# Output weights staged in freed operand slots, and their decode rows gathered into four events

## The chip, the cores and the metric

The kernel runs on one core of a Trainium2 chip, as one program and one launch. The metric is the device time of that core in microseconds (us). Engines are named as in the profile: PE is TensorE (matmuls), PEld its weight loads, DVE is VectorE, ACT is ScalarE, POOL is GpSimd and SP is SyncE, which here only issues DMAs.

## The reference, cut to what matters

One layer of a hybrid decoder. A normalised input of 1024 prompt tokens (and of 8 decode tokens beside them) goes through one projection; its columns feed two groups, an RG-LRU and an mLSTM of four heads worked in chunks of 128 tokens. The two outputs stand side by side, 2048 wide, and go through a second projection with `w_out` (2048 x 1024), then a last normalisation:

```python
u = hn @ w_in
...
yA, hA, bufA = rglru_branch(xa, conv0, h0, ...)
hB, C, n, m = mlstm_seq(q, k, v, ig, lf, C0, n0, m0)       # chunks of 128, carried state C, n, m
...
merged = jnp.concatenate([yA * silu(za), yB * silu(zb)], axis=-1)
x = x + merged @ w_out
y = rmsnorm(x, g_final)
```

`trunk` runs it once for the prompt and once for the decode tokens. All arrays are float32.

## The kernel before

Each float32 operand of a product is split into a high and a low part (`split`: hi is rounded by ACT, L70; lo is the remainder, by DVE, L71), and a product is three matmuls, hi x hi, hi x lo or lo x hi (`mm3`, L64 to L66). The framework orders each engine's instructions when the program is built, and each engine runs its own in that order and waits on the others by semaphores. Buffers come from pools by tag: a new tile of a tag takes the slot of an older one and waits until that is read. `ld` issues a DMA on SP's queue, `stq` one on POOL's.

**Phase 1, units.** The projection with `w_in` is 14 units of 512 output columns; the last is `z2z3`. Each unit is seven products (`product(u, q)`, q = 0 to 6), each of two halves of 12 matmuls of 512 columns. The operand of product q is the pair `cb[q]`, in big slots b(2q) and b(2q+1) of 4 KB x 2 a partition each. In the last unit these slots come free product by product. Weight halves (`wh`, `wl`) turn over in a pool `ws` of six slots of 4 KB a partition. Small background steps are popped after each half (`pop_bg`).

**w_out.** It is 16 blocks of 128 x 1024 (512 KB). Block m is loaded raw (`oraw`), split into the pair `wo[m]` for the prompt, and used raw for the decode tokens: `wo_prep` gives each half of a block a matmul (L1206) with the decode vector `mAd` (blocks 0 to 7, from the RG-LRU) or `mBd` (8 to 15, from the mLSTM) into one of four column groups of 32, so two blocks fill the four groups. Blocks 8 to 15 are scaled by a gain in the split (L1215, L1216).

**Staging before.** A raw block takes a `ws` slot. `wo_due(q)` runs after product q of the last unit, and appends the preparation of two blocks to the background after products 0 to 3. The split blocks 0 to 13 go to b0 to b13, 14 and 15 to the two raw slots of `w_in`. Blocks 8 to 11 are prepared after the last unit, 12 and 13 in chunk 1's first head and 14 and 15 in its second.

**Phase 2, chunks.** For chunk c and head h, n = 4c + h. Chunk 0 is computed in phase 1; the loop runs n = 4 to 31. `m_load` loads the decay row `W`, `qk` and `vt`; `m_k` (L1050 on `W`, then the splits `ql` and `Cl`) prepares; `m_a` (L1070, L1072) computes the scores; `pf` (L1079) multiplies them by `W`; `m_b` the chunk's products. `m_z` transposes two heads' outputs (L1176), multiplies with `z` and splits into `mh`, `ml`. W has three buffers, qk and vt two.

**Output parts.** `out_part(c, half, part)` is a generator: part 0 multiplies the r rows of chunk c (`rh`, `rl`, the RG-LRU's output from DRAM, loaded by `o_load(c)`) by blocks 0 to 7, part 1 the m rows (`mh`, `ml`) by blocks 8 to 15. They wait in the queue `work`, and `fill(k)` takes k steps of it, six matmuls each, between the chunk's own work:

```python
for k in range(8):
    w = wo[8 * part + k]
    mm3(x["p", half], mh[:, k, :], ml[:, k, :], w[:, 0, hs], w[:, 1, hs], part == 0 and k == 0, part == 1 and k == 7)
    if k % 2:
        yield
```

Of the kernel before, what the change touches and what calls it, by code (L numbers as in the profile page):

```python
# [9 lines left out]
F32 = mybir.dt.float32  # L10
F32R = mybir.dt.float32r
# [6 lines left out]
P = 128  # L18
T = 1024
# [30 lines left out]
def hymba_kernel(  # L50
# [7 lines left out]
    V, A, G, TE = nc.vector, nc.scalar, nc.gpsimd, nc.tensor  # L58
    ld = nc.sync.dma_start
# [8 lines left out]
    def split(hi, lo, src):  # L68

        A.copy(hi, src)  # L70
        V.tensor_tensor(lo, src, hi.bitcast(F32), op=ALU.subtract)  # L71
# [7 lines left out]
    def ps(tag, shape):  # L79
        return psp.tile(shape, F32, tag=tag, name=f"ps_{tag}", bufs=NBUF.get(tag, 1))  # L80

    def const(shape, name, dt=F32):
        return cpool.tile(shape, dt, tag=name, name=name)
# [3 lines left out]
    rawp = ctx.enter_context(tc.tile_pool(name="rawp", bufs=1))  # L87
# [3 lines left out]
    def big(n, shape, name, dt=F32R):  # L91
        return bpool.tile(shape, dt, tag=f"b{n}", name=name)

    def ws(shape, name, dt=F32R):

        return wsp.tile(shape, dt, tag="ws", name=name)
# [45 lines left out]
    mAd = const([P, 8, 32], "mAd")  # L142
# [51 lines left out]
    def run_late():  # L194
        now = late[:]
        late.clear()
        for f in now:
            f()
# [430 lines left out]
    bg, rgq, dcq = deque(), deque(), deque()  # L629
# [298 lines left out]
    mB = []  # L928
# [251 lines left out]
        split(x["mh"][:, s, :], x["ml"][:, s, :], z)  # L1180


    wo = []
    dec_o = []

    oraw = {}

    def wo_load(n):

        for m in (n, n + 1):  # L1190
            oraw[m] = ws([P, T], f"oraw{m}", F32)
            ld(oraw[m], w_out[0, m * P:(m + 1) * P, :])

    def wo_prep(n):


        if n == 0:
            dec_o.append(ps("tr", [P, 512]))
        if n not in oraw:
            wo_load(n)  # L1200
        for i in range(2):
            m = n + i
            md = mAd[:, m, :] if m < 8 else mB[0][:, m - 8, :]
            for half in range(2):
                g = 2 * i + half
                TE.matmul(dec_o[0][32 * g:32 * g + 32, :], md, oraw[m][:, half * 512:(half + 1) * 512], start=n == 0,  # L1206
                          stop=n == 14, skip_group_check=True)
        for m in (n, n + 1):
            raw = oraw.pop(m)
            t = big(m, [P, 2, T], f"wo{m}") if m < 14 else rawp.tile([P, 2, T], F32R, tag=f"raw{m - 14}", name=f"wo{m}")  # L1210
            if m < 8:
                split(t[:, 0], t[:, 1], raw)
            else:
                gm = gm4[:, m - 8:m - 7]
                A.mul(t[:, 0], raw, gm)  # L1215
                V.scalar_tensor_tensor(t[:, 1], raw, gm, t[:, 0].bitcast(F32), op0=ALU.mult, op1=ALU.subtract)  # L1216
            wo.append(t)

    def fms():
        return mx["p2"].tile([P, 4], F32, tag="fms", name="fms", bufs=2)  # L1220
# [42 lines left out]
    def o_load(c):  # L1263
        mh, ml = ws([P, 8, P], f"rh{c}"), ws([P, 8, P], f"rl{c}")
        for n, t in enumerate((mh, ml)):
            ld(t.bitcast(F32), d_rm[n, :, :, c * P:(c + 1) * P].rearrange("k p t -> p k t"))
        ot[c] = {"r": (mh, ml)}
# [71 lines left out]
    def fill(k):  # L1339
        for _ in range(k):  # L1340
            while work:
                if next(work[0], work) is work:
                    work.popleft()
                else:
                    break

    def wo_due(q):

        if q < 4:
            bg.append(lambda: wo_prep(2 * q))  # L1350
        if q == 6:
            bg.append(lambda: wo_load(8))


    seq = [(u, q) for u in range(1, len(units)) for q in range(7)]
    state = {"prep": 0, "m": False}
# [1 line left out]
    def preps(n):  # L1358
        while state["prep"] < min(n, len(seq)):
            prep(*seq[state["prep"]])  # L1360
            state["prep"] += 1
# [3 lines left out]
    last_u = len(units) - 1  # L1365
# [10 lines left out]
    part = 0  # L1376
    for n, (u, q) in enumerate(seq):
        preps(n + 1 + LEAD)
        for _ in product(u, q):
            pop_bg(2 if u == 1 or u == last_u else 1, 1, part % DEC[1 if u >= DEC[0] else 2] == 1)  # L1380
            part += 1
        if u == last_u:
            wo_due(q)
        if q == 6:
            for kind, j in units[u]:
                if kind == "x":
                    rg_unit(j)
            for half in range(2):
                if u == max(unit_of["v", 2 * half], unit_of["v", 2 * half + 1], 1):
                    bg.append(lambda half=half: dec_rows(half))  # L1390
            for h in range(NH):
                if done_h[h] == u:
                    bg.append(lambda h=h: dcq.extend(decode_steps(h)))
            if u == last_u - 1:
                dgen = decode_outputs()

                def step():
                    next(dgen, None)
                    run_late()
                state["out"] = [step] * 5 + [m_open2]  # L1400
        if not state["m"] and u > max(done_h) and not (bg or rgq or dcq or late):
            m_start()
        if u == last_u and q == 0:
            if not state["m"]:
                while bg or rgq or dcq or late:
                    pop_bg()
                m_start()
            bg.extend(state["out"])
# [3 lines left out]
    for n in range(2):  # L1412
# [1 line left out]

    work.extend([out_part(0, 0, 0), out_part(0, 1, 0), out_part(1, 0, 0), out_part(0, 0, 1), out_part(0, 1, 1),
                 out_part(1, 1, 0)])
    o_load(0)
    m_k(4)
    wo_load(10)
    wo_prep(8)  # L1420
    fill(2)
    wo_load(12)
    wo_prep(10)
    fill(2)
    N = 4 * NCH
    dend = dec_end()
    last = NCH - 1
    for n in range(4, N):
        c, h = n // 4, n % 4
        if h == 0 and c > 1:  # L1430
            work.extend([out_part(c, 0, 0), out_part(c - 1, 0, 1), out_part(c - 1, 1, 1)])
            work.append(out_part(c, 1, 0) if c < last else last_part(0))
        m_a(n)
        so_load(n)
        if n > 4:
            m_g(n - 1)
        m_load(n + 2)
        if h == 2 or n == 4:
            z_load(c if h == 2 else 0)
        if h == 0:  # L1440
            m_n(c - 1)
            fill(2)
            m_k(n + 1)
            fill(1)
            if c == 1:
                wo_prep(12)
                wo_load(14)
                o_load(1)
            m_b(n)
            fill(1)  # L1450
        elif h == 1:
            m_zg(c - 1)
            fill(1)
            m_k(n + 1)
            fill(1)
            m_z(c - 1, 0)
            if c == 1:
                wo_prep(14)
            m_b(n)
            fill(1)  # L1460
            m_z(c - 1, 1)
            fill(1)
            if c < last:
                o_load(c + 1)
        else:
            fill(1)
            tail()
            m_k(n + 1)
            fill(2)
            m_b(n)  # L1470
            fill(1)
        if c == 1 and h > 0:
            next(dend, None)
# [46 lines left out]
```

## Time and profile before

| | |
|---|---|
| time, median of 3 runs | 969.24 us (966.21 to 971.65) |
| span of the profiled execution, from its first to its last instruction | 973.6 us |
| mean granted TensorE clock | 0.989 of full speed |
| instructions | 15435 |
| ACT casts of blocks 0 to 7, L70 | 8 of 1.05 us |
| DVE remainders of blocks 0 to 7, L71 | 8 of 1.22 us |
| ACT and DVE for blocks 8 to 15, L1215 and L1216 | 8 of 1.15 us and 8 of 1.28 us |
| ACT's idle time ahead of L1215, for a block to land | 12.6 us, 6 times |

The profiled execution is one more than the three timed ones; no other time of its own than its span is given, and it lies 4.4 us above their median. In rows of the timeline the columns are start and length in us, the engine, line and operation, and the tiles out<-in. Matmuls overlap: one of 512 columns is listed with 0.39 us and the next starts 0.23 us after it, so starts are to be compared, not lengths.

### The profile page before, as it was taken

What the parts mean: (1) busy time and instruction counts of PE and PEld (TensorE: products, weight loads), DVE (VectorE), ACT (ScalarE), POOL (GpSimd) and SP (SyncE); (2) the same over time, 40 slices, a digit from 0 to 9 for tenths busy, and PEclk for the clock granted to TensorE, in tenths of its full rate; (3) what the DMA queues carried; (4) which work ended last, traced back from release to release, by engine and by line L of the source; (5) the groups of instructions that cost most, each with busy time, mean ns of one, the idle gap of its engine ahead of it and who ended that gap; (6) DMA issues with size and microseconds to landing.
All of it is one profiled execution on the core that took longest, in us unless ns stands there. A gap on an engine that the chain in (4) does not pass through costs nothing.

```text
span 973.6 us, 15435 instructions
## 1 busy us (share of the span) xinstructions
PE 940.9 (97%) x5378; PEld 765.3 (79%) x5378; DVE 715.7 (74%) x1482; ACT 584.7 (60%) x1044; POOL 146.2 (15%) x258
## 2 busy tenths in 40 slices
PE   7999998999999999999999999999899999999997
PEld 7887766777787987677889897876477888888886
DVE  6776798889898878787796846576565776666764
ACT  5553436778777777654777844646445466456643
POOL 1111112112212122202221211010100100000020
PEclk9999999999999999999999999999999999999999
DMA  5431446355745555447645463425963744564471
GB/s 190 136 125 43 130 125 229 137 190 188 260 143 198 179 174 173 158 126 241 197 155 163 153 183 101 132 81 172 296 209 105 204 136 128 154 176 140 118 114 52
DMA packets 131363, 153.71 MB, mean 158 GB/s; under 512 B 15798, under 2 KB 110038, under 8 KB 131278
## 3 DMA queue, kind: packets, MB, share of 16 engines
q1 hardware_dynamic: 113558, 96.86, 34.2%
q0 software_dynamic: 17728, 55.87, 16.1%
q8 instruction: 42, 0.69, 0.4%
q14 instruction: 35, 0.29, 0.1%
HBM read 101.11 MB, written 51.65 MB: 157 GB/s over the span
## 4 chain that ended last, share of the span: by engine, by line
PE 65%; DVE 12%; DMA 10%; issue 9%; ACT 2%; POOL 1%; SPq 1%; ACTq 0%; DVEq 0%; POOLq 0%
PE ps_o L66 11%; PE ps_o L64 11%; PE ps_o L65 10%; PE ps_kv L64 7%; PE ps_kv L66 7%; PE ps_kv L65 7%; DMA W<-d_alpha 3%; PE ps_tr L227 2%; DMA raw<-in_w_in_dram 2%; DVE wl L71 2%; PE ps_tr L1206 1%; PE ps_s L738 1%; DMA oraw<-in_w_out_dram 1%; PE ps_s L1070 1%; PE ps_qp L904 1%
## 5 line engine op out<-in xcount | busy, mean ns | idle before, releaser
L70 ACT CAST wh<-raw 128x1024 fp32r<-128x1024 f32 x91 | 95.3, 1049 | 62.0 <-PE ps_o L65 22.7
L71 DVE TENSOR_TENSOR wl<-raw,wh 128x1024 fp32r<-128x1024 f32 x91 | 110.9, 1219 | 26.3 <-ACT wh L70 14.7
L64 PE MATMUL ps_kv<-cb_hi,wh 128*128 128x512 f32 x320 | 128.3, 401 | 0.2 <-ACT s L308 0.2
L66 PE MATMUL ps_kv<-cb_hi,wl 128*128 128x512 f32 x320 | 126.2, 394 | 0.0
L65 PE MATMUL ps_kv<-cb_lo,wh 128*128 128x512 f32 x320 | 125.3, 392 | 0.0
L64 PE MATMUL ps_o<-cb_hi,wh 128*128 128x512 f32 x240 | 95.6, 398 | 0.0
L66 PE MATMUL ps_o<-cb_hi,wl 128*128 128x512 f32 x240 | 94.6, 394 | 0.0
L65 PE MATMUL ps_o<-cb_lo,wh 128*128 128x512 f32 x240 | 94.0, 392 | 0.0
L64 PEld LDWEIGHTS ps_kv<-cb_hi,wh 128*128 128x128 f32 x320 | 60.4, 189 | 24.5 <-issue 5.1
L66 PEld LDWEIGHTS ps_kv<-cb_hi,wl 128*128 128x128 f32 x320 | 60.3, 189 | 15.6 <-issue 2.5
L65 PEld LDWEIGHTS ps_kv<-cb_lo,wh 128*128 128x128 f32 x320 | 60.3, 188 | 11.9
L64 PE MATMUL ps_o<-wo,rh 128*128 128x512 f32 (+1 forms) x136 | 53.9, 396 | 1.7 <-DMA rh<-d_rm 1.7
L64 PE MATMUL ps_kv<-wh,cb_hi 128*128 128x256 f32 x192 | 55.3, 288 | 0.0
L65 PE MATMUL ps_kv<-wl,cb_hi 128*128 128x256 f32 x192 | 54.3, 283 | 0.0
L66 PE MATMUL ps_kv<-wh,cb_lo 128*128 128x256 f32 x192 | 54.3, 283 | 0.0
L64 PEld LDWEIGHTS ps_o<-cb_hi,wh 128*128 128x128 f32 x240 | 45.5, 189 | 10.9 <-issue 1.7
L66 PEld LDWEIGHTS ps_o<-cb_hi,wl 128*128 128x128 f32 x240 | 45.4, 189 | 10.7 <-issue 0.8
L66 PE MATMUL ps_o<-wo,ml 128*128 128x512 f32 (+1 forms) x136 | 52.3, 385 | 0.8 <-DVE ml L71 0.7
L64 PE MATMUL ps_o<-wo,mh 128*128 128x512 f32 (+1 forms) x136 | 52.9, 389 | 0.0
L65 PEld LDWEIGHTS ps_o<-cb_lo,wh 128*128 128x128 f32 x240 | 45.5, 190 | 9.3
L66 PE MATMUL ps_o<-wo,rl 128*128 128x512 f32 (+1 forms) x136 | 52.2, 384 | 0.1
L65 PE MATMUL ps_o<-wo,rh 128*128 128x512 f32 (+1 forms) x136 | 52.1, 383 | 0.0
(470 smaller groups left out, 2546.7 us busy)
## 6 DMA issues: line engine op xcount, KB each, us to landing
raw<-in_w_in_dram SPq DMA_DIRECT2D x56, 512.0 KB
Cb<-in_state_mlstm_C_dram SPq DMA_DIRECT2D x32, 256.0 KB
out_dram<-Cb POOLq DMA_DIRECT2D x32, 256.0 KB, 4.4
qk<-d_qk SPq DMA_DIRECT2D x32, 256.0 KB
oraw<-in_w_out_dram SPq DMA_DIRECT2D x16, 512.0 KB
d_qk<-s POOLq DMA_DIRECT2D x24, 256.0 KB, 3.5
x<-in_x_prompt_dram SPq DMA_DIRECT2D x8, 512.0 KB
d_x<-s POOLq DMA_DIRECT2D x16, 256.0 KB, 3.0
```

What stands on the lines that cost most here:

```text
L64: TE.matmul(out, ah, bh, start=first, stop=False, skip_group_check=True)
L65: TE.matmul(out, ah, bl, start=False, stop=False, skip_group_check=True)
L66: TE.matmul(out, al, bh, start=False, stop=last, skip_group_check=True)
L70: A.copy(hi, src)
L71: V.tensor_tensor(lo, src, hi.bitcast(F32), op=ALU.subtract)
L227: TE.matmul(pz[32 * g:32 * g + 32, :], hnd[:, k, :], raws[u, k // 4][:, k % 4, :], start=k < 4, stop=k >= 4, skip_group_check=True)
L738: TE.matmul(pg, w[:, n, :], st["xx"][n], start=k == 0, stop=k == 1)
L904: TE.matmul(pq[32 * g:32 * g + 4, 0:256], qsel[:, kb, 4 * bb:4 * bb + 4], ds_["C", h * NB + bb][:, kb, :], start=False, stop=b == NB - 1)
L1070: TE.matmul(S, qk[:, 2 + kb, :], qk[:, kb, :], start=kb == 0, stop=kb == 1)
L1206: TE.matmul(dec_o[0][32 * g:32 * g + 32, :], md, oraw[m][:, half * 512:(half + 1) * 512], start=n == 0, stop=n == 14, skip_group_check=True)
```

## The change

- A raw block pair is loaded into a freed operand slot, b0 or b1, as one tile of two blocks (`wo_load(n, slot)`); only 12 to 15 still use `ws` slots. Since b0 and b1 are needed for staging, split block m goes to b(m + 2), 12 and 13 to the raw slots and 14 and 15 to b0 and b1.
- `wo_prep` becomes `wo_dec` (decode rows of several blocks at once) and `wo_split`. `wo_due(i)` now runs inside the last unit after each of its 14 halves, and directly, not through the background queue: loads at halves 1, 6 and 11, decode rows of blocks 0 to 3 at half 4 and of 4 to 7 at half 9.
- The decode rows of blocks 8 to 13 and of 14 and 15 are two more events, behind the last unit. All splits stand ahead of the chunk loop.
- `o_load(0)` moves into the last unit, `o_load(1)` ahead of the loop, so r rows of two chunks are loaded then. The fills ahead of the loop are 2 and 3 steps instead of 2 and 2.

```diff
--- before.py
+++ after.py
@@ -1180,41 +1180,48 @@
         split(x["mh"][:, s, :], x["ml"][:, s, :], z)
 
 
-    wo = []
+    wo = {}
     dec_o = []
-
     oraw = {}
 
-    def wo_load(n):
-
-        for m in (n, n + 1):
-            oraw[m] = ws([P, T], f"oraw{m}", F32)
+    def wo_load(n, slot=None):
+
+        for i, m in enumerate((n, n + 1)):
+            if slot is None:
+                oraw[m] = ws([P, T], f"oraw{m}", F32)
+            else:
+                if i == 0:
+                    pair = big(slot, [P, 2, T], f"oraw{m}", F32)
+                oraw[m] = pair[:, i]
             ld(oraw[m], w_out[0, m * P:(m + 1) * P, :])
 
-    def wo_prep(n):
-
-
-        if n == 0:
+    def wo_dec(ns, first=False, last=False):
+
+        if first:
             dec_o.append(ps("tr", [P, 512]))
-        if n not in oraw:
-            wo_load(n)
-        for i in range(2):
-            m = n + i
+        ms = [n + i for n in ns for i in range(2)]
+        for m in ms:
             md = mAd[:, m, :] if m < 8 else mB[0][:, m - 8, :]
             for half in range(2):
-                g = 2 * i + half
-                TE.matmul(dec_o[0][32 * g:32 * g + 32, :], md, oraw[m][:, half * 512:(half + 1) * 512], start=n == 0,
-                          stop=n == 14, skip_group_check=True)
+                g = 2 * (m % 2) + half
+                TE.matmul(dec_o[0][32 * g:32 * g + 32, :], md, oraw[m][:, half * 512:(half + 1) * 512],
+                          start=first and m in ms[:2], stop=last and m in ms[-2:], skip_group_check=True)
+
+    def wo_split(n):
+
         for m in (n, n + 1):
             raw = oraw.pop(m)
-            t = big(m, [P, 2, T], f"wo{m}") if m < 14 else rawp.tile([P, 2, T], F32R, tag=f"raw{m - 14}", name=f"wo{m}")
+            if m in (12, 13):
+                t = rawp.tile([P, 2, T], F32R, tag=f"raw{m - 12}", name=f"wo{m}")
+            else:
+                t = big(m + 2 if m < 12 else m - 14, [P, 2, T], f"wo{m}")
+            wo[m] = t
             if m < 8:
                 split(t[:, 0], t[:, 1], raw)
             else:
                 gm = gm4[:, m - 8:m - 7]
                 A.mul(t[:, 0], raw, gm)
                 V.scalar_tensor_tensor(t[:, 1], raw, gm, t[:, 0].bitcast(F32), op0=ALU.mult, op1=ALU.subtract)
-            wo.append(t)
 
     def fms():
         return mx["p2"].tile([P, 4], F32, tag="fms", name="fms", bufs=2)
@@ -1344,13 +1351,24 @@
                 else:
                     break
 
-    def wo_due(q):
-
-        if q < 4:
-            bg.append(lambda: wo_prep(2 * q))
-        if q == 6:
-            bg.append(lambda: wo_load(8))
-
+    def wo_due(i):
+
+        if i in (1, 6, 11):
+            for slot in range(2):
+                wo_load({1: 0, 6: 4, 11: 8}[i] + 2 * slot, slot)
+        if i == 4:
+            wo_dec((0, 2), True)
+            wo_split(0)
+        if i == 5:
+            wo_split(2)
+        if i == 9:
+            wo_dec((4, 6))
+            wo_split(4)
+        if i == 10:
+            o_load(0)
+            wo_split(6)
+        if i == 12:
+            wo_load(12)
 
     seq = [(u, q) for u in range(1, len(units)) for q in range(7)]
     state = {"prep": 0, "m": False}
@@ -1379,8 +1397,8 @@
         for _ in product(u, q):
             pop_bg(2 if u == 1 or u == last_u else 1, 1, part % DEC[1 if u >= DEC[0] else 2] == 1)
             part += 1
-        if u == last_u:
-            wo_due(q)
+            if u == last_u:
+                wo_due((part - 1) % 14)
         if q == 6:
             for kind, j in units[u]:
                 if kind == "x":
@@ -1414,14 +1432,16 @@
 
     work.extend([out_part(0, 0, 0), out_part(0, 1, 0), out_part(1, 0, 0), out_part(0, 0, 1), out_part(0, 1, 1),
                  out_part(1, 1, 0)])
-    o_load(0)
     m_k(4)
-    wo_load(10)
-    wo_prep(8)
+    wo_load(14)
     fill(2)
-    wo_load(12)
-    wo_prep(10)
-    fill(2)
+    wo_dec((8, 10, 12))
+    for n in (8, 12, 10):
+        wo_split(n)
+    o_load(1)
+    fill(3)
+    wo_dec((14,), last=True)
+    wo_split(14)
     N = 4 * NCH
     dend = dec_end()
     last = NCH - 1
@@ -1442,10 +1462,6 @@
             fill(2)
             m_k(n + 1)
             fill(1)
-            if c == 1:
-                wo_prep(12)
-                wo_load(14)
-                o_load(1)
             m_b(n)
             fill(1)
         elif h == 1:
@@ -1454,8 +1470,6 @@
             m_k(n + 1)
             fill(1)
             m_z(c - 1, 0)
-            if c == 1:
-                wo_prep(14)
             m_b(n)
             fill(1)
             m_z(c - 1, 1)
```

The matmul of L1206 is L1207 after, `o_load`'s DMA L1266 is L1273, the raw block's DMA L1192 is L1196, and the final scaling of y in L1237 is L1244. The rows below are each engine's instructions in order; a count (x4) is of instructions as written, a number behind a name is its buffer.

PE in the middle of the last unit, at the first decode rows, before (`mAd`, two blocks an event, here blocks 0 and 1; L984 and, after, L965 are other work on the decode tokens):

```order
L984 MATMUL ps_s<-idF,dworka 8x128 x3
L1206 MATMUL ps_tr<-oraw_6487,mAd 32x512 x2
L984 MATMUL ps_s<-idF,dworka 8x128
L64 MATMUL ps_o<-cb_hi_160,wh_2_6421 128x512
L65 MATMUL ps_o<-cb_lo_161,wh_2_6421 128x512
L66 MATMUL ps_o<-cb_hi_160,wl_2_6422 128x512
L1206 MATMUL ps_tr<-oraw_6489,mAd 32x512 x2
```

and after:

```order
L66 MATMUL ps_o<-cb_hi_160,wl_2_6422 128x512
L1207 MATMUL ps_tr<-oraw_6462,mAd 32x512 x4
L1207 MATMUL ps_tr<-oraw_6465,mAd 32x512
L965 MATMUL ps_s<-dworkb,ones 128x64
L1207 MATMUL ps_tr<-oraw_6465,mAd 32x512 x3
L64 MATMUL ps_o<-cb_hi_160,wh_2_6421 128x512
```

Eight decode matmuls of blocks 0 to 3 now stand together, with one other matmul among them, where those of two blocks stood as two pairs with three matmuls of the unit between them.

PE from the last unit's last matmul, before (oraw_6808 and 6810 are blocks 8 and 9):

```order
L66 MATMUL ps_kv<-cb_hi_168,wl_6_6687 128x512
L1206 MATMUL ps_tr<-oraw_6808,mBd 32x512 x2
L1206 MATMUL ps_tr<-oraw_6810,mBd 32x512 x2
L64 MATMUL ps_o<-wo_6495,rh_6816 128x512
L65 MATMUL ps_o<-wo_6495,rh_6816 128x512
L1070 MATMUL ps_s<-qk 128x128 x2
L1072 MATMUL ps_s<-idF,qk 128x128 x2
L64 MATMUL ps_o<-wo_6495,rh_6816 128x512
L66 MATMUL ps_o<-wo_6495,rl_6817 128x512
```

and after, 12 matmuls of r rows further on (oraw_6772 and 6775 are the pairs 8, 9 and 10, 11; 6796 and 6798 are blocks 12 and 13):

```order
L64 MATMUL ps_o<-wo_6635,rh_6745 128x512
L65 MATMUL ps_o<-wo_6635,rh_6745 128x512
L66 MATMUL ps_o<-wo_6635,rl_6746 128x512
L1207 MATMUL ps_tr<-oraw_6772,mBd 32x512 x4
L1207 MATMUL ps_tr<-oraw_6775,mBd 32x512 x4
L1207 MATMUL ps_tr<-oraw_6796,mBd 32x512 x2
L1207 MATMUL ps_tr<-oraw_6798,mBd 32x512 x2
L64 MATMUL ps_o<-wo_6722,rh_6745 128x512
L65 MATMUL ps_o<-wo_6722,rh_6745 128x512
```

The rows of six blocks stand together behind the first two fill steps, where those of two blocks stood ahead of them.

PE in chunk 4, from the last r rows of a part to the first m rows (L1176 transposes the second pair of heads; L1070 is m_a), before:

```order
L66 MATMUL ps_o<-wo_6669,rl_7936 128x512
L1176 MATMUL ps_qp<-idF,hh 128x128 x4
L64 MATMUL ps_o<-wo_6715,rh_7935 128x512
L65 MATMUL ps_o<-wo_6715,rh_7935 128x512
L66 MATMUL ps_o<-wo_6715,rl_7936 128x512
L64 MATMUL ps_o<-wo_6718,rh_7935 128x512
L65 MATMUL ps_o<-wo_6718,rh_7935 128x512
L66 MATMUL ps_o<-wo_6718,rl_7936 128x512
L1070 MATMUL ps_s<-qk 128x128 x2
L1072 MATMUL ps_s<-idF,qk 128x128 x2
L64 MATMUL ps_o<-wo_6838,mh_8161 128x512
L65 MATMUL ps_o<-wo_6838,mh_8161 128x512
```

and after:

```order
L66 MATMUL ps_o<-wo_6752,rl_7936 128x512
L1176 MATMUL ps_qp<-idF,hh 128x128 x4
L64 MATMUL ps_o<-wo_6861,mh_8171 128x512
L65 MATMUL ps_o<-wo_6861,mh_8171 128x512
L66 MATMUL ps_o<-wo_6861,ml_8172 128x512
L64 MATMUL ps_o<-wo_6864,mh_8171 128x512
L65 MATMUL ps_o<-wo_6864,mh_8171 128x512
L66 MATMUL ps_o<-wo_6864,ml_8172 128x512
L1070 MATMUL ps_s<-qk 128x128 x2
L1072 MATMUL ps_s<-idF,qk 128x128 x2
```

The six matmuls between L1176 and L1070 are now with mh and ml, where they were with rh and rl; the order is like this in each of the chunks 1 to 6.

DVE shortly ahead of that, from the work behind L1050 of one head to the next pf, before (pf is the multiplication with W after which that W buffer is free; y is output of an earlier chunk):

```order
L1237 SCALAR_TENSOR_TENSOR y_8060<-y_8060,fms,gf_6812 128x512
L1131 SCALAR_TENSOR_TENSOR Cf_5787<-Cf_5787,cs_b,ps_kv 128x258 x2
L71 TENSOR_TENSOR ql<-qk,qh 128x256
L1237 SCALAR_TENSOR_TENSOR y_8061<-y_8061,fms,gf_6813 128x512
L71 TENSOR_TENSOR Cl<-Cf_5788,Ch 128x516
L1133 TENSOR_TENSOR hh<-ps_tr,hh 128x257
L71 TENSOR_TENSOR vl<-vt,vh 128x256
L1079 SCALAR_TENSOR_TENSOR pf<-ps_s,W 128x128
```

and after:

```order
L186 TENSOR_TENSOR ms<-ms 128x4
L1050 SCALAR_TENSOR_TENSOR W<-W,be_t,maskT 128x128
L187 SCALAR_TENSOR_TENSOR ms<-ms 128x4
L188 SCALAR_TENSOR_TENSOR ms<-ms 128x4
L1131 SCALAR_TENSOR_TENSOR Cf_5787<-Cf_5787,cs_b,ps_kv 128x258 x2
L71 TENSOR_TENSOR ql<-qk,qh 128x256
L71 TENSOR_TENSOR Cl<-Cf_5788,Ch 128x516
L1133 TENSOR_TENSOR hh<-ps_tr,hh 128x257
L71 TENSOR_TENSOR vl<-vt,vh 128x256
L1146 COPY ms<-hh 128x1
L1148 SCALAR_TENSOR_TENSOR hh<-so,hh 128x256
L1079 SCALAR_TENSOR_TENSOR pf<-ps_s,W 128x128
```

The scaling of y no longer stands between L1050 and pf, and L1146 and L1148 stand ahead of pf instead of behind it.

## The prediction

> **What bounds the kernel now.** I read the page first (its busy times), then the table by stage around the change, then the timeline of TensorE in it, then who waits for the raw blocks and for the chunk loads.
>
> ```profile
> PE 940.9 (97%) x5378; PEld 765.3 (79%) x5378; DVE 715.7 (74%) x1482; ACT 584.7 (60%) x1044; POOL 146.2 (15%) x258
> 650.00:675.00 25.00, 24.88 (x112) 16.51 (x111) 17.29 (x44) 13.80 (x19) 1.61 (x3) 1.00 0.44 147
> 675.00:693.80 18.80, 18.80 (x81) 11.49 (x83) 12.16 (x15) 9.47 (x12) 2.19 (x4) 1.00 0.70 226
> 693.80:701.00 7.20, 5.24 (x28) 3.14 (x27) 4.52 (x7) 3.68 (x7) 2.70 (x5) 1.00 1.06 304
> 701.00:708.80 7.80, 5.87 (x18) 2.76 (x19) 3.84 (x3) 4.27 (x4) 1.11 (x2) 0.78 0.70 248
> 708.80:730.00 21.20, 21.15 (x115) 14.90 (x114) 12.98 (x28) 9.25 (x21) 0.56 (x1) 1.00 0.72 221
> 800.00:900.00 100.00, 99.00 (x562) 85.16 (x562) 67.83 (x211) 56.51 (x150) 6.54 (x12) 1.00 0.51 149
> 900.00:973.60 73.60, 66.89 (x403) 58.68 (x401) 43.89 (x132) 32.75 (x86) 8.45 (x13) 0.98 0.45 96
> ```
>
> The stage rows read: stretch, its length, busy time of PE, PEld, DVE, ACT, POOL, granted clock, DMA share, GB/s. TensorE is the bound nearly everywhere: 18.80 of 18.80 us busy at the end of the last unit, 99.00 of 100 in the chunks. So what counts is what TensorE spends on the change's own matmuls and where it stands still. It stands still at one place near the change: 693.8 to 708.8, where it is busy 5.24 + 5.87 of 15.00 us and the clock falls to 0.78. I call 693.76, where the last unit's last matmul has started and the first decode event after it begins, T0.
>
> **Decode rows.** Each block event (L1206) is an insertion between 512-column matmuls that otherwise start every 0.23 us:
>
> ```profile
> 669.36 0.39 PE L64 MATMUL ps_kv<-cb_hi,wh 128*128 128x512 f32 x1
> 669.59 0.39 PE L65 MATMUL ps_kv<-cb_lo,wh 128*128 128x512 f32 x1
> 669.90 1.05 PE L1206 MATMUL ps_tr<-oraw,mAd 128*32 128x512 f32 x4
> 670.89 0.50 PE L66 MATMUL ps_kv<-cb_hi,wl 128*128 128x512 f32 x1
> 671.22 0.39 PE L64 MATMUL ps_kv<-cb_hi,wh 128*128 128x512 f32 x1
> 693.76 1.06 PE L1206 MATMUL ps_tr<-oraw,mBd 128*32 128x512 f32 x8
> 719.19 1.05 PE L1206 MATMUL ps_tr<-oraw,mBd 128*32 128x512 f32 x2
> 723.21 1.06 PE L1206 MATMUL ps_tr<-oraw,mBd 128*32 128x512 f32 x6
> 641.77 1.85 PE ps_tr L227 x16
> L1206 PE MATMUL ps_tr<-oraw,mAd x32: 592/605/617, 659.1 to 688.9; 128*32 128x512 f32 x32
> L1206 PE MATMUL ps_tr<-oraw,mBd x32: 592/617/1062, 693.8 to 723.7; 128*32 128x512 f32 x32
> ```
>
> A record count is twice the number of matmuls. L65 to the second L64 takes 1.63 us instead of 2 x 0.23, so an insertion of two matmuls costs 1.17. One matmul (x2), two (x4), three (x6) and four (x8), each in column groups of its own, take 1.05 to 1.06 alike: the price is per wave, not per matmul. Another line's eight matmuls in four groups (x16) take 1.85, so a wave that follows a wave costs 0.93.
>
> Before has 14 waves: the 32 mAd records in eight of four ahead of T0, the 32 mBd records in six after it (693.76 x8, 701.07 x4, 703.98 x4, another x8, 719.19 x2, 723.21 x6). 14 x 1.17 = 16.4 us. After has four events of 2, 2, 3 and 1 waves; the first is broken by one other matmul (L965) after five of its eight, so I count three waves there: 4 x 1.17 + 5 x 0.93 = 9.3. Gain 7.1 us, all on the path, since TensorE is full where it falls (24.88 of 25.00; 18.80 of 18.80).
>
> **Stalls that go.**
>
> ```profile
> 696.54 0.50 PE L64 MATMUL ps_o<-wo,rh 128*128 128x512 f32 x1 [1.71 <-DMA rh<-d_rm]
> 701.07 1.05 PE L1206 MATMUL ps_tr<-oraw,mBd 128*32 128x512 f32 x4 [0.23 <-DMA oraw<-in_w_out_dram]
> 703.98 1.92 PE L1206 MATMUL ps_tr<-oraw,mBd 128*32 128x512 f32 x4 [1.86 <-DMA oraw<-in_w_out_dram]
> 705.84 0.79 PE L64 MATMUL ps_o<-wo,rh 128*128 128x512 f32 x1
> 706.43 0.63 PE L65 MATMUL ps_o<-wo,rh 128*128 128x512 f32 x1
> 706.85 0.63 PE L66 MATMUL ps_o<-wo,rl 128*128 128x512 f32 x1
> 687.87 0.38 SPq L1266 DMA_DIRECT2D rh<-d_rm  x1
> 690.54 0.38 SPq L1266 DMA_DIRECT2D rl<-d_rm  x1
> 693.64 3.16 SPq L1192 DMA_DIRECT2D oraw<-in_w_out_dram  x4
> ```
>
> The brackets are TensorE's idle time and what ended it. The wait for chunk 0's r rows goes, because their loads, issued at 687.87 and 690.54, 6 and 3 us ahead of T0, move to the eleventh half of 14 in that unit, one place ahead of blocks 8 to 13. The two waits for blocks go, because blocks 10 to 13, issued from 693.64, go out before T0. That is 1.71 + 0.23 + 1.86 = 3.8. After the 1.86 the wave took 1.92 instead of 1.05, and the next starts lie 0.59 and 0.42 apart instead of 0.23: 0.87 + 0.36 + 0.19 = 1.4 of half clock that go with the wait.
>
> The Trainium skill (TensorE: Matmul & The Clock Gate, Part 1, "What's actually happening") says that the clock halves only after a whole idle window of about 3.4 us. No idle stretch here is longer than 1.86 us, so the trace differs; by the page the slow matmuls would have another cause, the 1.4 would stay, and the time would be 963.5 instead of 962.1. The trace decides for me: the slow rows stand right behind the wait.
>
> Together 7.1 + 3.8 + 1.4 = 12.3 us. The six wo matmuls of the third fill are only moved ahead of the loop (6 x 0.23 = 1.4). They come back as the end of the work queue, where TensorE is not the bound (66.89 of 73.60 us): between 0 and all of 1.4 of the gain is lost there. I take half: 11.6.
>
> **What the change adds.** (a) *Late blocks.* The third event needs blocks 8 to 13, queued on SP behind rh and rl of chunk 0: eight transfers of 512 KB, released as slots come free over the last five halves of the unit (a half is 12 x 0.228 = 2.74 us). T0 moves from 693.76 to about 689.5 (eight inserted waves, 9.4 us, against 3.0 + 2.1), so the first goes out near 675.8; the last is needed after 12 matmuls and two waves, near 694.3. 18.5 us for eight: at 226 GB/s (the row 675 to 693.8) a block takes 2.32 and all take 18.6; at 304 GB/s 13.8. No wait, or, if the last two are released late, up to one block's 2.3. I take 0.6, since the rate row stands right at the edge. Blocks 14 and 15 have 18 matmuls (4.1 us) more: 0 to 1, taken 0.3. The broken first event waits for DVE work that now stands behind splits of 1.2 us: 0 to 1.2, taken 0.3. Sum 1.2.
>
> (b) *Splits.* The splits of blocks 8 to 15 on ACT and DVE all stand ahead of the chunk loop, same in number and size. Their results are first used with chunk 1's m rows (730.7 below, some ten less after the change), more than 15 us after the last block's slot comes free at T0 plus a transfer: nothing. On SP chunk 1's z, qk and W loads stand behind rh and rl of chunk 1, which wait for the split of blocks 12 and 13, near 700; before, z went out at 707.00: nothing.
>
> ```profile
> L66 PE MATMUL ps_o<-wo,ml x136: 279/393/504, 730.7 to 966.7; 128*128 128x512 f32 x120, 128*128 128x256 f32 x16
> 707.00 0.38 SPq L1042 DMA_DIRECT2D z<-d_zs  x1
> ```
>
> (c) *The fill that runs one ahead.* It moves the chunk loop. Where TensorE did six matmuls of r rows between the transposes L1176 and m_a (L1070), it now goes at once to the products with mh and ml, then m_a. It therefore wants ml earlier, by 6 x 0.23 + 0.67 = 2.05 us. That order recurs in chunks 1 to 6. And ml stands on DVE behind a load:
>
> ```profile
> 825.65 0.28 DVE L1079 SCALAR_TENSOR_TENSOR pf<-ps_s,W 128x128 f32<-128x128 f32 x1
> 826.17 0.43 SPq L1023 DMA_DIRECT2D W<-d_alpha  x1
> 830.55 0.60 PE L1176 MATMUL ps_qp<-idF,hh 128*128 128x128 f32 x4
> 831.72 0.35 DVE L1050 SCALAR_TENSOR_TENSOR W<-W,be_t,maskT 128x128 f32<-128x128 f32 x1 [3.46 <-DMA W<-d_alpha]
> 832.38 0.60 PE L1070 MATMUL ps_s<-qk 128*128 128x128 f32 x4
> 833.32 0.68 DVE L71 TENSOR_TENSOR ml<-z,mh 128x512 fp32r<-128x512 f32 x1
> 834.06 0.50 PE L66 MATMUL ps_o<-wo,ml 128*128 128x512 f32 x1 [0.39 <-DVE ml L71]
> 800.53 0.50 PE L66 MATMUL ps_o<-wo,ml 128*128 128x512 f32 x1 [0.31 <-DVE ml L71]
> 823.71 0.74 DVE L1237 SCALAR_TENSOR_TENSOR y<-y,fms,gf 128x512 f32<-128x512 f32 x1
> PE ps_o L66 <- DVE ml L71: 0.7, 2, 0.4
> ```
>
> The wait is already there in two chunks (0.31 and 0.39, the only ones by the sum row): pf frees a W buffer, SP issues the load 0.5 us later, it lands 5.5 us later, and ql, Cf, Cl and ml follow. In the new order the two L1237 operations on y (0.67 each) stand earlier on DVE, ahead of the previous W wait, so pf and with it the load come up to 1.4 us sooner. Net 2.05 - 1.4 = 0.65 more stall per chunk. In chunks 3 to 6 the load stands ahead of ml in DVE's order: 4 x 0.65 = 2.6. In chunk 1 too, with less known: 0.1 to 1.4, taken 0.7. In 2 no load stands between. Bounds per chunk: 0 (DVE moves up by everything) to 2.05 (pf doesn't come sooner). I lean to the low side because pf's row has no bracket: DVE came to it from other work, not from a wait, so taking 1.4 of that work out moves it. Behind the waiting ml stand hh and z on DVE, which TensorE wants only some ten matmuls later: nothing further.
>
> **The sum.** -11.6 + 1.2 + 2.6 + 0.7 = -7.1 on a span of 973.6. The profiled span lies 4.4 us above the median of the runs (969.24; 966.21 to 971.65); the terms are the same in both, so 962.1.
>
> **Rivals.** *The new wait eats it (other side).* pf does not come sooner, and each of the chunks 1 and 3 to 6 stalls by the full 2.05: 5 x 2.05 = 10.3, and -11.6 + 1.2 + 10.3 = -0.1, 969: no change. If the clock also halves behind each stall, as it did at 703.98, that adds 5 x 1.4 = 7: +6.9, 976. It ends slower once a chunk loses more than (11.6 - 1.2 + 4.8) / 5 = 3.0 us. For it: the load's 5.5 us. Against: after the 1.71 us wait at 696.54 the matmul took 0.50, as the one at 834.06 does, not 0.79 as at 705.84. The Trainium skill (same page, "A second HAM failure mode: psum-queue depth-cycling") says that frequent small idles can make the clock swing; the chunks now have two such of 0.3 to 0.4 at a clock of 1.00, so nothing shows it yet. Chance 0.16, of it 0.06 slower.
>
> *The chunks are not hurt.* The load comes early enough and ml keeps pace: -11.6 + 1.2 = -10.4, and -12.3 if no block is late either and nothing is lost at the end: 957 to 959. For it: before, only two of six chunks wait at all. Chance 0.20.
>
> *The blocks are late (the change does not do what it says).* DMA runs at 304 GB/s and share 1.06 in before's 693.8 to 701; if the earlier issue only makes transfers slower, the third event waits as long as before, 3.8 + 1.4: the sum loses 5.2 - 0.6 = 4.6: 966.7. For it: the share of 1.06; against: 0.44 and 0.70 in the unit, which is where the loads go. Chance 0.14.
>
> **Chances and range.** The forecast, -7.1, has 0.50; its own bounds are (a) 0 to 4.5, (c) 0 to 10.3, tail 0.7 either way. Within 0.5% is 4.85 us, about what a measurement of this kernel tells from no change. Of the forecast 0.42 is past that and 0.08 not; the uninjured chunks are all faster (0.20); late blocks 0.03 faster, 0.11 same; the new wait 0.01, 0.09, 0.06. Sum: faster 0.66, same 0.28, slower 0.06. The range takes in the good rival below (957, less 1 for the reading) and the new wait without half clock above (969): 956 to 970.
>
> **What will show it.** L1206's successor (L1207) in four clusters, nine waves or fewer, in some 9.3 us; T0 about 4 us earlier; no rh wait after it and at most a short one at the third event, clock 1.00 there; the chunk loop's first mh product some ten us sooner than 730 (12.3 less the 1.4 of moved matmuls and the 1.2 of waits). Then idle of about 1 us ahead of the ml products in chunks 3 to 6, behind L1050's W. Wrong it is if the third event waits over 3 us, if a chunk takes over 2 us longer than the present 33.5 (834.06 - 800.53), or if the clock falls in the chunks.

## The result and the profile after

The changed kernel takes 963.44 us (median of 6 runs, 961.51 to 967.5) against 969.64 of the kernel before (6 runs): ratio 0.994, interval [0.9916, 0.9965]. In a second series it took 960.73 (11 runs) against 969.31: ratio 0.9924 [0.9901, 0.9948]. Faster by 0.6 to 0.8%, or 6.2 to 8.6 us; 962.1 had been forecast. The profiled execution of the first series is the longest of its six: it took 967.5 with a span of 965.7.

The stages of after, cut where its last unit now ends (T0 is 688.55; columns as in the prediction's table):

```profile
650.00:675.00 25.00, 25.00 (x120) 18.43 (x119) 21.23 (x49) 15.70 (x22) 1.61 (x3) 1.00 0.62 212
675.00:688.80 13.80, 13.80 (x70) 9.99 (x69) 10.82 (x13) 8.61 (x11) 2.19 (x4) 1.00 0.89 319
688.80:704.00 15.20, 15.20 (x85) 9.92 (x84) 9.13 (x11) 8.84 (x11) 4.34 (x8) 1.00 1.04 343
704.00:725.00 21.00, 16.95 (x90) 13.85 (x89) 10.52 (x27) 7.25 (x20) 0.00 (x0) 0.92 0.35 95
900.00:965.70 65.70, 58.19 (x358) 51.70 (x356) 37.69 (x116) 28.80 (x77) 8.41 (x13) 0.98 0.27 81
```

The hole behind T0 is gone: 15.20 of 15.20 us busy at a clock of 1.00, with DMA at a share of 1.04. But a new hole stands 15 us later: 16.95 of 21.00 busy, clock 0.92. The waits of TensorE from there to the end, in the timeline, with one slow matmul (721.40):

```profile
708.57 0.39 PE L64 MATMUL ps_qp<-vh,ph 128*128 128x258 f32 x1 [1.76 <-ACT hh L1126]
719.91 0.50 PE L66 MATMUL ps_o<-wo,ml 128*128 128x512 f32 x1 [2.29 <-DVE ml L71]
721.40 0.78 PE L65 MATMUL ps_o<-wo,mh 128*128 128x512 f32 x1
753.63 0.63 PE L1176 MATMUL ps_s<-idF,hh 128*128 128x128 f32 x4 [0.33 <-DVE kl L1080]
792.16 0.50 PE L66 MATMUL ps_o<-wo,ml 128*128 128x512 f32 x1 [0.97 <-DVE ml L71]
858.67 0.50 PE L66 MATMUL ps_o<-wo,ml 128*128 128x512 f32 x1 [0.54 <-DVE ml L71]
947.70 0.50 PE L64 MATMUL ps_o<-wo,mh 128*128 128x512 f32 x1 [1.00 <-ACT mh L70]
```

1.76 + 2.29 us of idle time in chunk 1, and matmuls at half pace behind the second (0.78 for one that takes 0.39 elsewhere; clocks of 0.58 and 0.74 in the two stretches of 2.5 us from 720, so 2.5 x 0.42 + 2.5 x 0.26 = 1.7 us): 5.8 us together. Before, the hole behind T0 was 3.8 of idle time and, reckoned in the same way from its stage row (clock 0.78 over 7.80 us), 1.7 of slow clock, not the prediction's 1.4: 5.5 us. **What the change took away in one place came back in the next.** From T0 to its last matmul TensorE stands idle for 5.6 us before (273.26 - 267.63 busy) and for 6.9 after (270.36 - 263.46 busy). The gain that stayed is for the most part that of the decode waves:

```profile
L1207 PE MATMUL ps_tr<-oraw,mAd 128*32 128x512 f32 x32 | 4.9, 601 | 0.0
L1207 PE MATMUL ps_tr<-oraw,mBd 128*32 128x512 f32 x32 | 3.8, 598 | 0.0
```

and of before, in the same view by groups of instructions (busy us, mean ns, idle time ahead and what ended it):

```profile
L1206 PE MATMUL ps_tr<-oraw,mAd 128*32 128x512 f32 x32 | 8.4, 605 | 0.0
L1206 PE MATMUL ps_tr<-oraw,mBd 128*32 128x512 f32 x32 | 7.2, 662 | 2.1 <-DMA oraw<-in_w_out_dram 2.1
```

15.6 us before, 8.7 after; 0.9 of the difference is the one slow wave at 703.98. TensorE's busy time from the start of the last unit to the end falls by 8.7 us (4.6 in the unit, 4.2 behind T0); some 1.6 of that is in no term of the prediction, and where it comes from stays open.

Single executions of one kernel differ by several us ahead of the change already (last section), so stages are compared: from a group of matmuls near the start of the last unit (615.27 before, 615.06 after) to the unit's last matmul, and from there to the last matmul of all. The rows of before and of after:

```profile
615.27 0.60 PE L1070 MATMUL ps_s<-qk 128*128 128x128 f32 x4
693.45 0.39 PE L66 MATMUL ps_kv<-cb_hi,wl 128*128 128x512 f32 x1
966.71 0.28 PE L66 MATMUL ps_o<-wo,ml 128*128 128x256 f32 x1
```

```profile
615.06 0.60 PE L1070 MATMUL ps_s<-qk 128*128 128x128 f32 x4
688.55 0.39 PE L66 MATMUL ps_kv<-cb_hi,wl 128*128 128x512 f32 x1
958.91 0.28 PE L66 MATMUL ps_o<-wo,ml 128*128 128x256 f32 x1
```

The same three rows give this for every kernel run (the experiments follow). The time is the median of a kernel's runs. Each series has its own runs of before, to which the ratio refers: medians of 969.64 for after, 969.31 for after_again to late_w_op, 970.08 for late_w_mark to late_w_late_r and 969.12 for the last two. One of the seven runs of serial_groups, 1146.13 us at a clock of 0.75, is a slow run that the ratio leaves out; the median of the other six is 961.7.

| kernel | last unit, us | T0 to the end, us | time, us | ratio to before |
|---|---|---|---|---|
| before | 78.18 | 273.26 | 969.64 | |
| after | 73.49 | 270.36 | 963.44 | 0.994 [0.9916, 0.9965] |
| after_again | 73.48 | 269.82 | 960.73 | 0.9924 [0.9901, 0.9948] |
| fill_2_2 | 73.49 | 270.64 | 962.27 | 0.994 [0.9918, 0.9961] |
| serial_groups | 74.38 | 269.39 | 962.03 | 0.9935 [0.991, 0.996] |
| late_w_op | 73.49 | 261.55 | 950.57 | 0.9816 [0.979, 0.9843] |
| late_w_mark | 73.49 | 261.55 | 951.24 | 0.9809 [0.9785, 0.9833] |
| before_late_w | 78.27 | 268.99 | 964.86 | 0.9943 [0.9919, 0.9967] |
| late_w_single | 77.93 | 261.66 | 955.55 | 0.985 [0.9825, 0.9874] |
| late_w_late_r | 73.49 | 268.02 | 957.54 | 0.9873 [0.9847, 0.9899] |
| late_w_serial | 74.38 | 264.20 | 953.89 | 0.9836 [0.9811, 0.9862] |
| late_w_fill_2_2 | 73.49 | 260.75 | 951.39 | 0.9805 [0.9777, 0.9833] |

By these stages the change gains 7.6 us in after (4.69 + 2.90) and 8.1 in after_again (4.70 + 3.44); 7.1 had been forecast.

### The profile page after: what moved, and what is told of

It reads as the page before. It is cut to its first block, busy times and chain, and to the rows that moved or that the text cites. A ratio compares the mean times of both kernels' runs of the same rounds, so it can differ in the third digit from the quotient of the medians.

```text
span 965.7 us, 15416 instructions
## 1 busy us (share of the span) xinstructions
PE 933.2 (97%) x5378; PEld 766.5 (79%) x5378; DVE 718.2 (74%) x1482; ACT 581.9 (60%) x1044; POOL 146.1 (15%) x258
## 4 chain that ended last, share of the span: by engine, by line
PE 68%; DVE 9%; issue 8%; DMA 7%; ACT 4%; POOL 1%; SPq 1%; POOLq 0%; ACTq 0%; DVEq 0%
PE ps_o L66 12%; PE ps_o L64 12%; PE ps_o L65 12%; PE ps_kv L64 7%; PE ps_kv L65 7%; PE ps_kv L66 7%; PE ps_tr L227 2%; DMA W<-d_alpha 2%; DVE wl L71 1%; PE ps_s L1070 1%; PE ps_s L738 1%; DMA Cb<-in_state_mlstm_C_dram 1%; DMA rh<-d_rm 1%; PE ps_tr L1207 1%; DMA raw<-in_w_in_dram 1%
## 5 line engine op out<-in xcount | busy, mean ns | idle before, releaser
L64 PE MATMUL ps_o<-wo,mh 128*128 128x512 f32 (+1 forms) x136 | 53.5, 394 | 1.0 <-ACT mh L70 1.0
L64 PE MATMUL ps_o<-wo,rh 128*128 128x512 f32 (+1 forms) x136 | 52.9, 389 | 0.0
L65 PE MATMUL ps_o<-wo,mh 128*128 128x512 f32 (+1 forms) x136 | 51.9, 382 | 0.0
```

Of the source, the lines that this page charges most:

```text
L64: TE.matmul(out, ah, bh, start=first, stop=False, skip_group_check=True)
L65: TE.matmul(out, ah, bl, start=False, stop=False, skip_group_check=True)
```

## The experiments

**What the wait in chunk 1 hangs on.** Other engines of after, in the timeline around the first of the two waits (SP, DVE, ACT):

```profile
701.09 0.29 DVE L1079 SCALAR_TENSOR_TENSOR pf<-ps_s,W 128x128 f32<-128x128 f32 x1 [2.52 <-ACT kh L1078]
701.41 0.33 SPq L1023 DMA_DIRECT2D W<-d_alpha  x1
706.63 0.35 DVE L1050 SCALAR_TENSOR_TENSOR W<-W,be_t,maskT 128x128 f32<-128x128 f32 x1 [4.59 <-DMA W<-d_alpha]
707.01 0.31 ACT L1051 ACTIVATE W<-W 128x128 f32<-128x128 f32 x1 [5.30 <-DVE W L1050]
708.05 0.47 ACT L1126 ACTIVATE hh<-ps_qp,gi_t 128x257 f32<-128x257 f32 x1
717.56 0.35 DVE L1050 SCALAR_TENSOR_TENSOR W<-W,be_t,maskT 128x128 f32<-128x128 f32 x1 [3.09 <-DMA W<-d_alpha]
719.17 0.68 DVE L71 TENSOR_TENSOR ml<-z,mh 128x512 fp32r<-128x512 f32 x1
```

pf of head n = 4 frees a W buffer at 701.4; the load into it lands 5.2 us later. Behind that pf, DVE's order has L1050 on just that buffer, for n = 7, which is needed three heads later:

```
L1079 SCALAR_TENSOR_TENSOR pf_6917<-ps_s_6912,W_6590 128x128          (n = 4)
L1080 SCALAR_TENSOR_TENSOR kl_6921<-ps_s_6912,de_t_99,kh_6920 128x256
L71 TENSOR_TENSOR pl_6919<-pf_6917,ph_6918 128x128
L1050 SCALAR_TENSOR_TENSOR W_7032<-W_7032,be_t_98,maskT_85 128x128    (n = 7, for the pf three further on)
L71 TENSOR_TENSOR ql_6965<-qk_6598,qh_6964 128x256
```

DVE runs in order and stands still, ACT's L1051 with it; and ACT's L1126, which reads the accumulator that TensorE's next product writes (ps_qp in chunk 1), is queued behind L1051. That is the 1.76. The second wait is the same for n = 8 (L1050 at 717.56), with ml behind it. This is the theory; the rival is that the extra fill step makes TensorE ask too early.

First the changed kernel once more.

> The changed kernel once more, as the mark for the others on the same chip. Theory (the gain is the decode waves; what the removed stalls gave came back in chunk 1 behind W's load): -6 us against before, 963 to 964, with TensorE idle 1.8 us ahead of an m_b product and 2.3 us ahead of ml in chunk 1, and slow matmuls behind the second. Rival (the chunk 1 stalls are an accident of one execution): the new profile shows less than 1 us of them, and 959.

```profile
702.47 0.39 PE L64 MATMUL ps_qp<-vh,ph 128*128 128x258 f32 x1 [1.89 <-ACT hh L1126]
714.72 0.50 PE L66 MATMUL ps_o<-wo,ml 128*128 128x512 f32 x1 [1.59 <-DVE ml L71]
851.87 0.50 PE L66 MATMUL ps_o<-wo,ml 128*128 128x512 f32 x1 [1.62 <-DVE ml L71]
702.50:705.00 2.50, 2.50 (x12) 2.26 (x13) 1.94 (x6) 0.41 (x1) 0.00 (x0) 0.67 0.00 0
705.00:707.50 2.50, 2.50 (x9) 2.05 (x8) 0.94 (x3) 1.13 (x4) 0.00 (x0) 0.65 0.51 146
```

960.73 us. Both waits are there again (1.89 and 1.59), this time with the slow clock behind the first: 2.5 x 0.33 + 2.5 x 0.35 = 1.7. So the stalls are no accident of one execution.

**The W operation placed later.** L1050 now writes a tile of its own, which has one buffer, so it cannot start before the pf of the head before. The raw tile that the load fills has two buffers instead of three, and L1050 frees them:

```diff
-        W = mx["p"].tile([P, L], F32, tag="W", name="W", bufs=3)
+        W = mx["p"].tile([P, L], F32, tag="W", name="W", bufs=2)
...
-        W = d["W"]
-        V.scalar_tensor_tensor(W, W, be_t[:, c, h:h + 1], maskT, op0=ALU.add, op1=ALU.min)
+        W = mx["p"].tile([P, L], F32, tag="Wd", name="Wd")
+        V.scalar_tensor_tensor(W, d["W"], be_t[:, c, h:h + 1], maskT, op0=ALU.add, op1=ALU.min)
+        d["W"] = W
```

> L1050 writes a tile of its own with one buffer, so head n's W operation can't stand on DVE before head n-1's pf; W's raw buffers are 2. Theory: DVE's and ACT's waits for W (30.4 us) fall below 5, both chunk 1 stalls (1.76 and 2.29) and the 1.7 of slow clock go, and the 0.97 and 0.54 in chunks 3 and 5: 6 to 7 us below the changed kernel, 956 to 958. Rival (the extra fill step makes TensorE want ml too early whatever W does): DVE's wait goes, but 3 us or more of TensorE's waits stay, on z, mh or Cl: 961 to 963.

```profile
PE ps_o L64 <- ACT mh L70: 1.0, 1, 1.0
695.00 0.29 DVE L1080 SCALAR_TENSOR_TENSOR pf<-ps_s,Wd 128x128 f32<-128x128 f32 x1 [1.87 <-ACT kh L1079]
695.87 0.34 DVE L1050 SCALAR_TENSOR_TENSOR Wd<-W,be_t,maskT 128x128 f32<-128x128 f32 x1
696.24 0.33 SPq L1023 DMA_DIRECT2D W<-d_alpha  x1
```

950.57 us, 10.2 below after_again; the first row is all that TensorE waits for from 640 on, and DVE reaches L1050 without a bracket. ACT still waits 9.7 us for the W operation behind T0, in 15 pieces of at most 0.7, where below 5 was expected; TensorE waits for none of it. The edit also changes what frees the load's buffer, but the load does not go out sooner: here W's load is issued 1.24 us behind the start of n = 4's pf (696.24 against 695.00), in after 0.32 (701.41 against 701.09). What differs is which L1050 stands behind that pf: here that of n = 5, whose W landed long ago; the one for n = 7, which needs this load, comes two heads later. The stage behind T0 shortens by 8.27. Counted from T0, the first group of products with mh comes 3.6 us sooner than in after_again (1.89 and the 1.7), the second a further 2.4 (the 1.59 stands between them), and the sixth a further 1.9 (the 1.62, in chunk 5): 7.9 of the 8.3 stand where the waits stood. The theory holds; its 6 to 7 us were 1.3 us too few by the stage and 3 by the medians. This version is faster than both kernels and needs no more memory.

**The fill step undone.**

```diff
-    fill(3)
+    fill(2)
```

> The fills ahead of the loop are 2 and 2 again, all else as changed. Theory (W's operation stands too early on DVE and ACT): the hh wait of about 1.8 us in chunk 1 stays, since it does not hang on the fill; the ml wait shrinks by about 2 and the slow clock behind it goes, chunks 3 to 6 wait 0.3 to 0.4 twice as before: 960 to 963. Rival (the fill step is the cause): all of chunk 1's 5.8 us go, 957 to 959. By the prediction's own step (0.65 per chunk and 0.7): 3.3 less, 960.

```profile
710.37 0.39 PE L64 MATMUL ps_qp<-vh,ph 128*128 128x258 f32 x1 [3.48 <-ACT hh L1126]
722.17 1.08 PE L1176 MATMUL ps_qp<-idF,hh 128*128 128x128 f32 x4 [2.23 <-DVE hh L1133]
```

962.27 us, stage 270.64: nothing gained. In chunk 1 the ml wait goes, but the hh wait grows from 1.8 to 3.5 and another (2.23) opens behind the second L1050, and the slow clock, which was expected to go, stands behind that one (0.50 from 722.25 to 725.67, 1.7 us). So the time fell into the range expected, but not in the way expected. TensorE comes to the same late operation by another way, and the rival falls: chunk 1 loses 7.4 us without the fill step, 5.8 with it. In the later chunks TensorE waits 0.4 for ml in all, against 1.5 in after (0.97 + 0.54), so there the step costs about 1.1, where the prediction had 2.6.

**Decode matmuls in another order.** Neighbours share a column group (the line that sets `md` moves inward too):

```diff
-        for m in ms:
-            for half in range(2):
-                g = 2 * (m % 2) + half
+        for g in range(4):
+            for m in ms:
+                if m % 2 != g // 2:
+                    continue
+                half = g % 2
```

> The decode matmuls of an event in another order: all those of one column group in a row, so that neighbours share a group. Same matmuls, same data, same loads. Theory (the price is per wave of different groups): eight matmuls take 5 waves instead of 2 and twelve take 9 instead of 3, 12 more waves of 0.93: 11 us more than the changed kernel, 974 to 975. Rival (the price is per event or per matmul, whatever the group): no difference, 963 to 964.

```profile
653.42 1.90 PE L1209 MATMUL ps_tr<-oraw,mAd 128*32 128x512 f32 x4
655.62 1.93 PE L1209 MATMUL ps_tr<-oraw,mAd 128*32 128x512 f32 x12
672.22 1.94 PE L1209 MATMUL ps_tr<-oraw,mAd 128*32 128x512 f32 x16
687.96 5.43 PE L1209 MATMUL ps_tr<-oraw,mBd 128*32 128x512 f32 x24
717.18 0.50 PE L66 MATMUL ps_o<-wo,ml 128*128 128x512 f32 x1 [2.43 <-DVE ml L71]
```

962.03 us: the theory missed by 12 us or more, and the rival's time nearly came, but not for its reason. By the rows the order does cost: with the last event's 1.06, which is the same, 12.3 us against 8.7. Two matmuls of one group (x4) take 1.90, two waves; twelve take 5.43 instead of 2.78. But eight take 1.94, as in the good order (1.92), so some of them must have overlapped with others that don't stand next to them. "A wave for each pair of neighbours" was too strict, and why twelve overlap so much less than eight is left open. The time rose by 1.3 at most. The hh wait in chunk 1 (1.89 in after_again) is gone and no slow clock follows, while the ml wait is longer (2.43 against 1.59): what TensorE lost ahead of the late W operation it no longer waited there.

**On ground where that wait is gone.** The next five kernels all have the later W operation.

> The changed kernel with the later W operation once more, as the mark for the next three: 950 to 952, no TensorE wait but the 1.0 us for mh at the end.

951.24 us, the mark. The kernel before with the same edit:

> The kernel before with the same edit of W. Theory (the change removed waits for blocks and r rows which W's wait then gave back, while before W's wait is mostly hidden behind those): before gains only what it waits behind W now, 0.3 + 0.4 + 0.6 + 0.2 us and small pieces, 1.5 to 4: 965 to 968; so on this ground the change is worth 15 to 17 us instead of 6 to 8. Rival (W's operation costs both kernels the same): 8 to 10 us less, 959 to 961.

```profile
690.19 0.50 PE L64 MATMUL ps_o<-wo,rh 128*128 128x512 f32 x1 [1.63 <-DMA rh<-d_rm]
709.19 0.39 PE L64 MATMUL ps_qp<-vh,ph 128*128 128x258 f32 x1 [2.63 <-ACT hh L1127]
706.79 1.15 ACT L1216 ACTIVATE wo<-oraw,gm 128x1024 fp32r<-128x1024 f32 x1 [4.69 <-DMA oraw<-in_w_out_dram]
```

964.86 us: before gains 5.2, more than the 1.5 to 4 expected, less than the rival's 8 to 10. The change is then worth 964.86 - 951.24 = 13.6 us (by stages 4.8 + 7.4 = 12.2) instead of 6 to 9 (by stages 7.6 to 8.1): not the 15 to 17 expected, but about half as much again as it shows, by the stages. The rows say why before still loses time: the r rows are late (1.63), and ACT stands 4.69 us at a late block with hh queued behind it (2.63). With the change and the later W neither wait is there.

Decode rows of blocks 0 to 7 one block at a time (the calls; `wo_dec` takes single blocks then):

```diff
-        if i == 4:
-            wo_dec((0, 2), True)
-            wo_split(0)
-        if i == 5:
-            wo_split(2)
-        if i == 9:
-            wo_dec((4, 6))
-            wo_split(4)
+        if 4 <= i < 12:
+            wo_dec((i - 4,), i)          # one block
+        if i in (5, 7, 9, 11):
+            wo_split(i - 5)
```

> Changed kernel with the later W operation; the decode rows of blocks 0 to 7 in eight insertions of one block, one a half, instead of two events; splits of those blocks at most two halves later. Theory (1.17 us for an insertion, 0.93 for a wave behind it): 8 x 1.17 = 9.4 against 5.1, 4 us more, 954 to 956. Rival (it is absorbed, as the serial order was): at most 1.5 us more, 951 to 952.

```profile
657.27 1.05 PE L1208 MATMUL ps_tr<-oraw,mAd 128*32 128x512 f32 x4
```

955.55 us, 4.3 more; the last unit grows by 4.44 and nothing else moves. As expected.

Chunk 0's r rows loaded behind the unit:

```diff
         if i == 10:
-            o_load(0)
             wo_split(6)
...
+    o_load(0)
     m_k(4)
```

> Changed kernel with the later W operation; chunk 0's r rows are loaded behind the last unit's loop as before, on SP now behind blocks 8 to 13. Theory (the early load of r removes a wait of TensorE): a wait on rh of 2 to 6 us behind the last unit, with slow matmuls after it in some executions: 953 to 958. Rival (r rows arrive in time also then): 950 to 952.

```profile
683.62 0.57 PE L64 MATMUL ps_o<-wo,rh 128*128 128x512 f32 x1 [3.37 <-DMA rh<-d_rm]
682.50:685.00 2.50, 1.38 (x6) 0.78 1.05 301
685.00:687.50 2.50, 2.50 (x10) 0.53 0.99 379
```

957.54 us, 6.3 more: 3.37 of wait, about 1.7 of half clock (0.78 and 0.53 in TensorE's own table by stretches), and the third event in two pieces (3.27 and 1.92, the first at half clock, against 2.78 in one). As expected.

The serial order again:

> The later W operation together with the serial order of the decode matmuls. On the changed kernel that order cost 3.5 us in its own rows (12.3 against 8.7), yet 1.3 in the time. Theory (whatever TensorE saves or loses ahead of W's wait in chunk 1 is taken up by that wait): without the wait the 3.5 us come through, 954 to 955.5. Rival (the rows overstate the cost): 951 to 952.5.

953.89 us. The last unit grows by 0.89 and the rest by 2.65, together the 3.5 us of the rows, of which the kernel with the W wait showed 0.5 in its stages (+0.89 and -0.43). By the medians it is 2.7, just below the range expected; but the two kernels ran on two chips, and against each chip's own before it is 3.6.

> The later W operation with fills of 2 and 2 ahead of the loop. Theory (the third fill step made no wait of its own, W's operation did): no wait of TensorE for ml with either, 950 to 952.5, the moved matmuls worth at most 1.4 at the end. Rival (the fill step wants ml about 2 us too early, 0.65 a chunk): 2.5 to 4 less, 947 to 949.

951.39 us: no difference in the time, and no wait for ml with either; 0.8 less behind T0, where the 1.0 us wait for mh at the end is gone.

## Why the prediction was right, and where it was not

The time was right, to 1.3 us in the first series and 1.4 in the second. The mechanism was right for the gain and wrong for the new loss; that the sum came out is in part luck. Its steps:

- **Decode waves**, 16.4 to 9.3: measured 15.6 to 8.7 in their rows, and 4.69 less in the last unit, where 9.4 - 5.1 = 4.3 was worked out. A wave behind a wave cost 0.86 (2.78 for three waves, 1.92 for two) instead of 0.93. The first event was broken by L965, as the order showed, and took 1.90 + 1.06. late_w_single shows the price of an insertion, late_w_serial that the order within an event counts.
- **Stalls that go**, 3.8 and 1.4 of half clock: all gone behind T0; the half clock was worth 1.7. For the r rows late_w_late_r shows it; for the blocks no run takes the early loads away.
- **(a) Late blocks**, 1.2: nothing. No wait at any of the four events, and DMA moved 319 and 343 GB/s there (share 0.89 and 1.04), where the term stood on 226.
- **(b) Splits**, nothing: no wait for a split block in after.
- **(c) The fill step** failed, in chunk 1 by size and mechanism: 0.7 was allowed, 5.8 us came (1.76 + 2.29 + 1.7 of clock). The step looked for a W load ahead of ml alone, and priced it by how much sooner TensorE asks. The L1050 that stands right behind pf also holds up ACT's hh, and late_w_op shows that W's operation is the cause, fill_2_2 that the fill step isn't. From chunk 2 on, 2.6 was forecast and 0.3 came: waits of 0.97, 0.54 and 0.33 in after (1.62 and 0.2 in after_again), against 0.31 and 0.39 for ml and two at L1176, 0.8 together, before. By the prediction's own sign ("if the clock falls in the chunks") this step was wrong: it fell in chunk 1.
- **The end**, 0.7: about right. TensorE now waits 1.00 for mh there, and 0.8 of the stage goes with the fill step (late_w_fill_2_2).

So the sum came out because errors cancel: (a) and (c) together were forecast at 0.7 + 2.6 + 1.2 = 4.5 and cost 5.8 + 0.3 = 6.1, and the gain was larger than forecast by somewhat more, about 2 us, of which 1.6 is in no term. The rival of the new wait was right in kind: W's load did eat what the removed stalls gave, but in chunk 1 alone, and not by way of the new order. Its half clock behind a stall was there too, once behind T0 in each of the two profiles of the changed kernel.

The prediction weighed the clock rule of the Trainium skill (TensorE: Matmul & The Clock Gate, Part 1, "What's actually happening") against the 1.86 us wait. The runs bear out the trace: late_w_late_r, after, fill_2_2 and after_again have half clock behind waits of 3.4, 2.3, 2.2 and 1.9 us, of which only the first comes near the page's window of 3.4.

## What to carry to other kernels

Work that an engine saves ahead of a wait is worth nothing until the wait goes: here over a third of a change's gain (some 4 of 12.2 us by the stages) sat behind an operation that a static order had placed three heads early, right behind the buffer's release, with a 5 us load between. Look on each in-order engine for operations that stand directly behind the release of the buffer they wait for, and hold them back with a tile of their own. Compare stages between fixed rows, not spans, where single executions scatter by more than the effect.

## What the runs showed of the hardware

**The clock falls in stretches of one length.** The clock record that is kept with each trace has TensorE at half clock in stretches of 3.41 us (once of twice that, and longer when its work is done), and within one execution their starts lie whole multiples of 3.413 us apart; where that grid lies differs from execution to execution. So a stretch in which TensorE is busy throughout costs 3.41 / 2 = 1.7 us. Many have nothing to do with the change: before T0 there are four in after (from 17.25, 30.91, 406.37 and 607.76) and none in after_again, 4 x 1.7 = 6.8 us, and the two profiles reach T0 at 688.55 and 682.32, 6.2 us apart.

**What decides is not the length of a wait, but how it falls into that grid.** TensorE's own table, cut at the grid's edges (stretch, length, busy time, clock, DMA share, GB/s), around the two waits of after in chunk 1:

```profile
706.75:710.16 3.41, 1.65 (x11) 1.00 0.00 0
710.16:713.57 3.41, 3.41 (x21) 1.00 0.59 164
716.99:720.40 3.41, 1.12 (x5) 1.00 0.63 164
720.40:723.81 3.41, 3.41 (x15) 0.50 0.13 39
```

and around the longest wait of fill_2_2, 3.48 us:

```profile
705.19:708.60 3.41, 1.70 (x12) 1.00 0.33 96
708.60:712.01 3.41, 1.64 (x11) 1.00 0.00 0
712.01:715.43 3.42, 3.42 (x21) 1.00 0.54 161
```

The 3.48 us are shared by two windows, each with 1.6 to 1.7 us of work left, and the clock stays. The 1.89 us of after_again lie in one window, which keeps 1.52, and the next has half clock. Behind T0, in all twelve profiles, half clock came behind each window with 1.52 us of work or less and behind none with 1.57 or more. This is no rule for the whole kernel: ahead of T0 it also came behind windows with up to 2.4 us of work.

A window that runs free of the program is what the Trainium skill states in the section named above (TensorE: Matmul & The Clock Gate, Part 1, "What's actually happening"), with the same 3.4 us. These records agree with that. They do not agree that a whole window has to be idle: one that was busy for 1.52 of its 3.41 us was enough.
